# Short-sequence attention on one core: which queue issues the output stores, and when

## Chip, cores and metric

The kernel runs on one core of a Trainium2 chip. The metric is the device time of one execution in microseconds; the figure for a kernel is the median of several runs. A profile is of one single execution.

## What is computed

Batch 32, 12 heads, 128 positions, head size 64, all f32 in and out; 384 independent heads in all.

```
scale = 1.0 / np.sqrt(q.shape[-1])
scores = scale * np.matmul(q, k.transpose(0, 1, 3, 2))
attn = np.exp(scores - scores.max(-1, keepdims=True))
attn = attn / (attn.sum(-1, keepdims=True) + 1e-8)
return np.matmul(attn, v).astype(np.float32)
```

Three inputs of 12.58 MB each are read and one output of 12.58 MB is written.

## The kernel before

**Tiling.** The work is cut into 48 *units* of eight heads (NU, L32). Four units make a *super-unit* (supers, L35): 12 of them, numbered 0 to 11. For each super-unit there is one load of q, one of k and one of v, 1 MB of f32 each, turned into bf16 by the transfer (512 KB as written). q and k have four buffers each (NQ), v has two (NVB).

**A unit's way.** VectorE copies q or k into pairs of heads (pair_up, L248). TensorE transposes these (L174) and VectorE copies the transposes back (L257). TensorE puts v in order by matmuls with a selection matrix (order_v, "V", L188), and ScalarE copies that to SBUF (L234). TensorE makes the scores (L214), ScalarE the exponentials (L239), and TensorE multiplies by v, with a column of ones that gives the sums (L226). VectorE takes the reciprocal of the sums (L266) and multiplies (normalise, "N", L269), which leaves a unit's output in an o_sb tile of its own chunk; no o_sb tile is used twice.

**Order.** Each engine's instructions are laid down by hand in a list (program), and semaphores come from the dependencies. The steps in L409 to L434 run the units one behind the other in a software pipeline: step u has the V of unit u + 3, the scores of u + 1, the values of u and the N of u - 1.

**Loads.** All 36 loads are issued by GpSimd, in the order q, k, v of a super-unit (L436 to L446). Its queue is in order: an instruction that waits holds everything behind it. A q or k load waits until the buffer's last reader, four super-units ago, is done; a v load of super-unit x waits until V has read super-unit x - 2 (L387). Since the v load comes ahead of the next q and k in the queue, its wait paces all loads.

**Stores.** The 48 units' outputs are stored in 26 *chunks* (stores, L59): two chunks of one unit, 22 of two units, two of one unit. A chunk of two units is stored by two transfers (pieces, L351), so there are 48 store transfers of 256 KB each. The list own (L356) holds the chunks that GpSimd issues: before, those up to unit 33 (OWN = 34), 18 chunks and 34 transfers. The other eight chunks, 14 transfers, are issued by SyncE. A chunk of GpSimd's waits for the N of its last unit; one of SyncE's also waits for the N of unit 40 (HELD, L381). lane (L358) picks one of eight semaphores on which a chunk's transfers count their landing, four for each of the two issuers; SyncE waits for all eight at the end (L556).

**Where the stores stand in GpSimd's queue.** Behind each k load of super-unit x, chunks are added while the units stored so far, the next chunk's included, are at most MIXED * (x - 4) / 7 (L447, with MIXED = 24). So the first ones come with super-unit 5, and 24 units are stored ahead of the last v load. The rest of GpSimd's chunks follow behind the last load.

Of the kernel before, what the change touches and what calls it, by code (L numbers as in the profile page):

```python
# [10 lines left out]
def kernel(  # L11
# [23 lines left out]
    supers, u0 = [], 0  # L35
# [23 lines left out]
    stores = [1, 1] + [2] * ((NU - 4) // 2) + [1, 1]  # L59
# [26 lines left out]
    MIXED, OWN, HELD = 24, 34, NU - 8  # L86
# [267 lines left out]
        return 2 if 1 < stores[c] < supers[of_unit[first]][0] // 4 else 1  # L354

    own = [c for c in range(len(stores)) if sum(stores[:c + 1]) <= OWN]  # L356

    def lane(c):  # L358

        return c % 4 + (4 if c in own else 0)  # L360

    def store(c):
        name = "POOL" if c in own else "SP"
        e = ENGINE[name]
        n = stores[c]
        first = sum(stores[:c])
        R, f = supers[of_unit[first]]
        J = R // 4

        def emit():  # L370
            dst = o_rows[:, 2 * f:2 * f + 2 * J, :].rearrange("p (a w) e -> p a w e", a=2)[
                :, :, first - f:first - f + n, :]
            src = o_sb[c][:].rearrange("p (a w e) -> p a w e", a=2, w=n)
            if pieces(c) == 1:
                e.dma_start(out=dst, in_=src).then_inc(s_o[lane(c)], 16)  # L375
            else:
                for a in range(2):
                    e.dma_start(out=dst[:, a], in_=src[:, a]).then_inc(s_o[lane(c)], 16)  # L378

        last = first + n - 1  # L380
        op(name, ("store", c), emit, [("N", last if c in own else max(last, HELD))])  # L381

    def pool_load(kind, x):
        deps = []
        if kind == "v":
            if x >= NVB:
                deps = [("V", sum(vgroups[:x - NVB + 1]) - 1)]  # L387
            n, first = vgroups[x], sum(vgroups[:x])
            op("POOL", ("load", kind, x), lambda: nc.gpsimd.dma_start(  # L389
                out=v_b[x % NVB][:, :n, :], in_=v_rows[:, first:first + n, :],  # L390
            ).then_inc(s_v[x % NVB], 16), deps)
            return
        R, f = supers[x]
        j = "qk".index(kind)
        rows, bufs, sm = ((q_rows, q_b, s_q), (k_rows, k_b, s_k))[j]
        if x >= NQ:
            deps = [("P", t) for t in t_order if t[0] == x - NQ and t[1] == j]
        n = f * 8 // R

        def emit():  # L400
            nc.gpsimd.dma_start(  # L401
                out=bufs[x % NQ][:], in_=rows[R][:, n:n + 2, :]).then_inc(sm[x % NQ], 16)

        op("POOL", ("load", kind, x), emit, deps)
# [39 lines left out]
    todo = list(range(len(stores)))  # L444
    for _, kind, x in loads:
        pool_load(kind, x)  # L446
        while kind == "k" and sum(stores[:todo[0] + 1]) <= MIXED * (x - 4) / (len(supers) - 5):  # L447
            store(todo.pop(0))
    for c in todo:
        store(c)  # L450
# [138 lines left out]
```

The softmax here doesn't subtract the row's maximum and nothing guards it: scores larger than these inputs give would overflow.

## Time and profile before

| | us |
|---|---|
| median of 5 runs | 134.71 |
| the runs | 132.42, 132.71, 134.71, 135.47, 135.12 |
| the profiled execution | 135.38 |
| its span, first to last instruction | 133.6 |

| engine | busy us | share of the span |
|---|---|---|
| TensorE matmuls | 95.5 | 71% |
| VectorE | 89.6 | 67% |
| ScalarE | 73.7 | 55% |
| GpSimd | 51.1 | 38% |

The page cuts the span into 40 slices of 3.34 us and gives the busy share of each in tenths. A transfer's issue has a start on the issuing engine, and a landing, when its semaphore has its full count; between them lie the waiting in the queue and the transfer itself. The medians from issue to landing are 11.6 us for q, 13.4 for k, 10.5 for v, 12.8 for GpSimd's stores and 5.1 for SyncE's. GpSimd issues its 36 loads and 34 stores at 0.71 to 0.82 us each; SyncE issues its 14 stores from 114.3 us on. The share of the DMA engines in windows can be above 1, since packets overlap on an engine.

### The profile page before, as it was taken

To read this page: it belongs to the slowest core of one execution; us is meant where nothing else is said; L and a number is where in the kernel's file an instruction comes from. 1 tells how busy PE (TensorE), PEld (TensorE's weight loads), DVE (VectorE), ACT (ScalarE), POOL (GpSimd) and SP (SyncE) were. 2 spreads that over 40 slices of the span, in tenths; PEclk is the share of its full clock that TensorE was granted. 3 is DMA by queue.
4 is the path that set the end of the run, shared out by engine and by line. 5 is a ranking of instruction groups with operands and counts; after the bars stand their busy time and mean duration, and the time that the engine had idled before them with its cause. 6 is when DMAs were issued, how large, how long until landed. Compare 5 with 4: busy or idle time off the path is not lost. (4 is left out here: it accounts for less than half of the span.)

```text
span 133.6 us, 6988 instructions
## 1 busy us (share of the span) xinstructions
PE 95.5 (71%) x3072; PEld 67.7 (51%) x3072; DVE 89.6 (67%) x204; ACT 73.7 (55%) x97; POOL 51.1 (38%) x75
## 2 busy tenths in 40 slices
PE   0035889999899989888499589887688578577400
PEld 0034466776676666656366367555455456354200
DVE  1144535998989979599279489699198398475520
ACT  0001536868776785754655574971853754779400
POOL 5930004224073490953700941935904980000000
PEclk9999999999999999999869999999999999999955
DMA  1999999999999999999999999999999999999960
GB/s 12 165 198 207 211 204 214 162 192 202 205 211 181 196 267 229 208 347 227 211 343 230 211 284 213 243 326 207 240 328 216 239 327 317 405 383 342 329 210 10
DMA packets 19400, 31.56 MB, mean 236 GB/s; under 512 B 1344, under 2 KB 11072, under 8 KB 19392
## 3 DMA queue, kind: packets, MB, share of 16 engines
q0 software_dynamic: 15584, 27.79, 97.1%
q1 hardware_dynamic: 3808, 3.67, 8.0%
q8 instruction: 4, 0.07, 0.2%
q14 instruction: 4, 0.03, 0.1%
HBM read 37.75 MB, written 12.58 MB: 377 GB/s over the span
## 5 line engine op out<-in xcount | busy, mean ns | idle before, releaser
L239 ACT ACTIVATE attnT<-s_ps 128x1024 bf16<-128x1024 f32 x48 | 49.4, 1029 | 0.4 <-PE s_ps L214 0.2
L234 ACT CAST v_e<-v_ps 128x512 bf16<-128x512 f32 x48 | 28.3, 589 | 38.3 <-PE v_ps L188 19.7
L174 PE MATMUL qk_ps<-ident,pair 128*128 128x128 bf16 x384 | 32.3, 232 | 15.3 <-PEq L467 15.3
L188 PE MATMUL v_ps<-v_b,sel 128*32 128x256 bf16 x768 | 31.9, 289 | 11.4 <-PEq L467 11.3
L257 DVE COPY qkT<-qk_ps 128x1024 bf16<-128x1024 bf16 x48 | 32.8, 684 | 5.5 <-PE qk_ps L174 4.5
L269 DVE TENSOR_TENSOR o_sb<-o_ps,recip 128x512 f32<-128x512 f32 x48 | 33.2, 691 | 1.7
L174 PEld LDWEIGHTS qk_ps<-ident,pair 128*128 128x128 bf16 x384 | 24.0, 103 | 19.9 <-issue 18.5
L389 POOL DMA_DIRECT2D v_b<-in_v_dram x12 | 9.3, 774 | 57.3 <-PE v_ps L188 57.3
L188 PEld LDWEIGHTS v_ps<-v_b,sel 128*32 128x32 bf16 x768 | 16.9, 99 | 18.0 <-issue 14.0
L226 PE MATMUL o_ps<-v_e,attnT 128*32 128x65 bf16 x1536 | 21.0, 196 | 4.2 <-PEq L467 3.6
L248 DVE COPY pair<-q_b 128x1024 bf16<-128x1024 bf16 x24 | 10.9, 453 | 18.2 <-DMA q_b<-in_q_dram 18.1
L378 POOL DMA_DIRECT2D out_dram<-o_sb x32 | 23.0, 733 | 0.0
L226 PEld LDWEIGHTS o_ps<-v_e,attnT 128*32 128x32 bf16 x1536 | 15.5, 97 | 10.1 <-issue 6.5
L214 PE MATMUL s_ps<-qkT 64*128 64x128 bf16 x384 | 19.7, 224 | 0.7 <-PEq L467 0.5
L214 PEld LDWEIGHTS s_ps<-qkT 64*128 64x128 bf16 x384 | 11.2, 96 | 11.2 <-issue 11.2
L266 DVE RECIPROCAL recip<-o_ps 128x8 f32<-128x8 f32 x48 | 9.7, 202 | 8.7 <-PE o_ps L226 8.1
L248 DVE COPY pair<-k_b 128x1024 bf16<-128x1024 bf16 x24 | 10.3, 427 | 1.4 <-DMA k_b<-in_k_dram 1.4
L401 POOL DMA_DIRECT2D q_b<-in_q_dram x12 | 8.7, 727 | 1.0 <-SPq L94 1.0
L401 POOL DMA_DIRECT2D k_b<-in_k_dram x12 | 8.7, 727 | 0.0
L234 ACT ACT_TABLE_LOAD x1 | 1.3, 1283 | 13.0 <-DMA v_b<-in_v_dram 13.0
L546 DVE COPY sel<-ident 128x128 bf16<-128x128 bf16 x2 | 0.4, 223 | 1.8 <-POOL ident L521 1.8
L375 POOL DMA_DIRECT2D out_dram<-o_sb x2 | 1.4, 730 | 0.0
(8 smaller groups left out, 1.4 us busy)
## 6 DMA issues: line engine op xcount, KB each, us to landing
out_dram<-o_sb POOLq DMA_DIRECT2D x34, 256.0 KB, 12.8
q_b<-in_q_dram POOLq DMA_DIRECT2D x12, 512.0 KB, 11.6
k_b<-in_k_dram POOLq DMA_DIRECT2D x12, 512.0 KB, 13.4
v_b<-in_v_dram POOLq DMA_DIRECT2D x12, 512.0 KB, 10.5
out_dram<-o_sb SPq DMA_DIRECT2D x14, 256.0 KB, 5.1
```

Of the source, the lines that this page charges most:

```text
L174: i = nc.tensor.transpose(p[:, :, r4, jj, :], x[:, r].rearrange("p a d -> p (a d)"), ident[:])
L188: x = nc.tensor.matmul(t[r4 * 32:(r4 + 1) * 32, i, :, :], lhsT=pick[:, w * nh + i, jv, :], rhs=v_b[g % NVB][:, :n, (4 * jv + r4) * D:(4 * ...
L214: i = nc.tensor.matmul(t[:, a, h, :], lhsT=x[p, 1, 4 * w + h, :], rhs=x[p, 0, 4 * w + h, :], start=True, stop=True)
L226: y = nc.tensor.matmul(t[h * SO:(h + 1) * SO, a, r * (D + 1):(r + 1) * (D + 1)], lhsT=x[:, a, h, r * SO:(r + 1) * SO], rhs=v_e[m % NVE][:, ...
L234: return nc.scalar.copy(v_e[m % NVE][:, :, :D], v_ps[:].rearrange("p (n e) -> p n e", e=D))
L239: return nc.scalar.activation(out=attnT[u % NA][:].rearrange("p a h (r s j) -> p (a h r) s j", r=4, j=J), in_=s_ps[u % 2][:].rearrange("p ...
L248: return nc.vector.tensor_copy(pair[t_index[t] % NP][:], src[:, 8 * b:8 * b + 8])
L257: return nc.vector.tensor_copy(x.rearrange("p h (r j s) -> p (h r) j s", r=4, j=J)[:, :, 2 * b:2 * b + 2, :].rearrange("p x j s -> p x (j ...
L266: nc.vector.reciprocal(r[:], o4[:, :, :, D]).then_inc(s_r, 1)
L269: return nc.vector.tensor_mul(o[:, :, w, :].rearrange("p a (r d) -> p a r d", d=D), o4[:, :, :, :D], r[:].unsqueeze(3).to_broadcast([128, ...
L378: e.dma_start(out=dst[:, a], in_=src[:, a]).then_inc(s_o[lane(c)], 16)
L401: nc.gpsimd.dma_start(out=bufs[x % NQ][:], in_=rows[R][:, n:n + 2, :]).then_inc(sm[x % NQ], 16)
```

## The change

Two edits. In own, every second chunk behind the last that GpSimd already has is added, without the last two chunks: these are the chunks numbered 19, 21 and 23, with units 36-37, 40-41 and 44-45. They go from SyncE's queue to the end of GpSimd's, wait for their own units alone, and count on GpSimd's semaphores. In the loop that puts stores among the loads, the bound becomes MIXED * (x - 3) / 8.

```diff
     own = [c for c in range(len(stores)) if sum(stores[:c + 1]) <= OWN]
+    own += range(own[-1] + 2, len(stores) - 2, 2)
...
     for _, kind, x in loads:
         pool_load(kind, x)
-        while kind == "k" and sum(stores[:todo[0] + 1]) <= MIXED * (x - 4) / (len(supers) - 5):
+        while kind == "k" and sum(stores[:todo[0] + 1]) <= MIXED * (x - 3) / (len(supers) - 4):
             store(todo.pop(0))
```

The store transfers in GpSimd's queue behind the k load of each super-unit:

| k load of super-unit | 4 | 5 | 6 | 7 | 8 | 9 | 10 | 11 | behind the last load |
|---|---|---|---|---|---|---|---|---|---|
| before | 0 | 2 | 4 | 4 | 2 | 4 | 4 | 4 | 10 |
| after | 2 | 4 | 2 | 4 | 2 | 4 | 2 | 4 | 16 |

GpSimd then issues 40 store transfers and SyncE 8.

## The prediction

> **What bounds the kernel now.** I read the slices first, then the DMA queues, then the waits, then the tail in finer windows. From the page:
>
> ```profile
> PE   0035889999899989888499589887688578577400
> DVE  1144535998989979599279489699198398475520
> DMA  1999999999999999999999999999999999999960
> GB/s 12 165 198 207 211 204 214 162 192 202 205 211 181 196 267 229 208 347 227 211 343 230 211 284 213 243 326 207 240 328 216 239 327 317 405 383 342 329 210 10
> ...
> q0 software_dynamic: 15584, 27.79, 97.1%
> q1 hardware_dynamic: 3808, 3.67, 8.0%
> ...
> HBM read 37.75 MB, written 12.58 MB: 377 GB/s over the span
> ```
>
> No compute engine holds a 9 throughout; the DMA row does, from the second slice to the 38th. GB/s counts bytes as written, so a load that turns f32 into bf16 shows half of what it reads: about 205 in load stretches is 410 read. Two slices of the first fifteen stand lower, 162 and 181. The second holds the interval that matters. GpSimd issued the k load of super-unit 4 at 30.8 us, landing 11.3 later (42.1); the next load, v of super-unit 4, was issued at 37.5 and landed 7.9 later (45.4). Those lie 3.3 us apart, where the q and k behind them (38.3 + 9.7 and 39.0 + 11.4) land 2.4 apart. So about **0.8 us** of transfer time went unused near 44 us: the queue ran dry. Finer windows of 0.2 us show rates of 133 to 179 GB/s there. Behind 45 us every group of loads has stores queued with it and v landings take 9.1 to 12.7 us: never dry again. Waits from 45 to 114.5 us:
>
> ```profile
> POOL v_b L389 <- PE v_ps L188: 31.8, 7, 7.6
> ACT v_e L234 <- DMA v_b<-in_v_dram: 17.6, 8, 3.1
> DVE pair L248 <- DMA q_b<-in_q_dram: 12.5, 7, 2.7
> ```
>
> The compute engines wait for landings; GpSimd waits only for the v buffer, never for a store's data. The last v load (issued 102.0, landing 12.4 later) ends the loads at 114.4, and ScalarE had idled 2.75 us for it. The rest takes 13.6 us, to the last VectorE multiply, which ends at 128.04. SyncE issues the last store at 128.1, landing 3.8 later (131.9); the span ends 1.7 after that. The last 4 us, in windows of 0.1 us:
>
> ```profile
> DMA  9941111000699999972000000000000000000000
> GB/s 328 338 144 41 51 51 41 21 31 20 236 358 358 348 348 338 358 267 62 31 20 20 21 31 20 31 20 20 31 21 20 31 20 20 31 20 0 0 0 0
> ```
>
> After most of the last store has gone (129.8), a trickle of 20 to 31 GB/s runs to 131.6: about one sixteenth of the rate above it, so one DMA engine with a backlog of 1.8 us. It also trickled at 128.3 to 129.0 while the others had nothing. **Two ends lie close together**: the compute tail behind the last v, and that engine's queue, which sets the end.
>
> **What the Trainium skill says.** "DMA: Bandwidth & Descriptors", section "Issuing engines are not separate DMA queues": transfers from SyncE and GpSimd run on the same 16 engines, and a second issuer saves only issue time. The trace agrees: the DMA row is 9 with GpSimd alone and when SyncE joins at 114.3. Its section "Latency and other measured facts" says that engines 7 and 15 are usually slower, its cause a guess; the trace shows one late engine, not which. Its section "Queues, rings and completion order" says that an engine takes turns between queues packet by packet: hence a SyncE store overtakes GpSimd's queue, while GpSimd's own stay in order. The trace fits: SyncE's store issued at 124.8 landed in 2.7 us, GpSimd's of 109.1 in 13.9.
>
> **The change, part by part.**
>
> *Stores among the loads.* Removed: nothing. Moved: GpSimd's first 24 store transfers. Counted behind the k load of super-units 4 to 11 they were 0, 2, 4, 4, 2, 4, 4, 4 and become 2, 4, 2, 4, 2, 4, 2, 4: in total ahead of the last v load, 24 both times. Summed up, 2 more stand ahead behind the k of 4, 4 more behind that of 5, 2 more behind those of 6 to 9, none from 10 on. Each costs GpSimd 0.72 us; it has 3.3 to 7.6 us of wait per group, which hides it (without that cover, at most 4 x 0.72 = 2.9 us in a group). Their data is old enough: the first two need units 0 and 1, long finished at 31.6 us; the two issued behind super-unit 11 are counted against units up to 23, while PE is past the V of unit 35. No new wait.
>
> In the transfer queue a store takes 262 KB / 405 GB/s = 0.65 us (the rate at 114.5 to 117.4 us, GpSimd's stores alone). The two early ones, 1.3 us, come behind k of 4 and fill the 0.8 us gap. The v of 4 and the q and k of 5 then land 1.3 - 0.8 = 0.5 us later; the v of 5 and the q and k of 6, with 4 more ahead, 4 x 0.65 - 0.8 = 1.8 later; from the v of 6 to the k of 10, with 2 more ahead, 0.5 later. From the v of 10 on the same bytes are ahead, so these come **0.8 us earlier**, the last v too. The lateness costs compute waiting, nothing at the end, if the queue does not run dry and compute catches up: the 2.75 us of idling before the last v shrinks by at most 0.8 + 0.5, leaving 1.4. Worth: -0.8 us on the compute tail and on the late engine's queue. Bounds: 0 if the dry spell moves elsewhere, -1.3 if the two stores fill all of their length.
>
> *Stores in turns.* The chunks of units 36-37, 40-41 and 44-45, 6 transfers, go from SyncE to GpSimd. SyncE keeps 8. GpSimd gets a new wait for each; behind the one for unit 37 stand only the other two chunks, and nobody waits for those but the end. Unit 37's multiply ends at 108.0, GpSimd is busy with its ten stores to 109.8, so no wait: these go out at 109.8 to 111.2 instead of 116.0 and 117.2, behind the last v in its queue, which they don't delay. The next pair goes at 117.8 (unit 41) instead of 120.8, the last at 124.8 (unit 45), as now. Issue on GpSimd is 1.45 us a pair, hidden, since it has nothing else; the second of the last pair leaves at 125.5. If GpSimd's own delay to the first packet is as at the start (issued 1.5, first packets near 3.1), it moves by 127.2 to 128, within the backlog. SyncE's issues took up to 1.22 us each and its chunk of units 40-41 was late by 3.1 (117.7 to 120.8); that goes, but transfers were queued on the engines, so it gains nothing by itself.
>
> What it can gain is transfer efficiency: SyncE's stores move at 347 GB/s in 120 to 125 us, 0.755 us each, against 0.65. Six times the difference is 0.65 us. Part of that lower rate is lack of work, so bounds are 0 and -0.65; below nothing not excluded: the larger packets of GpSimd's queue beside SyncE's could cost +0.3. I take half, **-0.3**.
>
> *Sum.* -0.8 - 0.3 = -1.1 us. The late engine then ends at 131.6 - 1.1 = 130.5. The compute limit is 127.3 for the last issue plus the shortest landing seen, 2.7: 130.0, so the engine still decides, just. Span 133.6 - 1.1 = 132.5; the profiled execution, 135.38, becomes 134.3. The median of the five runs, 134.71, lies 0.7 below the profiled one; on it the change gives **133.6**.
>
> **Rivals.**
> 1. *Faster, the backlog dissolves.* If GpSimd's earlier store issues also take off the 1.8 us lag of the one engine, the end falls onto compute: 0.8 plus that lag, 2.6 us, and with the 0.65 in full up to 3.2: 131.5 to 132.1. For: the lag is visible, and SyncE was late with chunks. Against: work on an engine is conserved, and the shortest landing leaves only 1.9 us of room. The spread of the five runs, 132.42 to 135.47, is as large as this.
> 2. *Slower, the loop of loads runs dry.* A q load is issued when PE frees the v buffer and its landing feeds VectorE; later loads delay V, and that delays the next issue. If at each of the six v loads from 5 to 10 the queue is empty when v is issued, each costs a gap like the early ones (0.8 us): 6 x 0.8 = 4.8, less 1.1: +3.7, 138.4. It decides once a v landing falls below about 8 us, as the one with the gap (7.9). Against: landings are 9.1 to 12.7 now and the stores add to what is queued.
> 3. *No gain.* The dry spell reappears, or the end is fixed by the late engine in another way: 134.7. That the edit does nothing is excluded by the count of issues: 40 and 8 for 34 and 14.
>
> **How the numbers follow.** Forecast, 133.6, own range 132.8 to 134.4: 0.56. Rival 1, 131.8: 0.20; no gain, 134.7: 0.10; slower, 138.4: 0.14. The range leaves out most of the slower case and the edge of the faster: **131.3 to 135.5**. The bound of 2% (about what a measurement of this kernel can tell from no change) is 132.0 and 137.4. Faster: of rival 1 0.17, and 0.13 of the forecast's and no-gain's cases through the spread: 0.30. Slower: 0.13 of rival 2 and 0.01: 0.14. Within: 0.56.
>
> **What would show it.** Right: GpSimd issues stores from about 31.6 us; v of super-unit 4 lands near 45.9, without a dry stretch before it; the last v lands near 113.6; ScalarE's wait before it stays over 1 us; the last trickle ends near 130.5. Wrong: v landings of 8 us or less behind 45 us; a store on GpSimd that waits for VectorE ahead of a load; the last v at or behind 114.4; SyncE's last landing over 4 us after its issue.

## The result and the profile after

The changed kernel takes **134.15 us** in the median of 42 runs, the kernel before 133.79 in the median of 79. The ratio is **1.0036, 95% interval 1.0013 to 1.0059**: 0.13 to 0.59% slower, where 0.8% faster was forecast. The ratios, here and below, leave out the executions that lie more than 1.5% above their kernel's fastest, and the medians do not. The profile after is of an execution of 132.62 us (span 130.8), that of before of one of 135.38 us (133.6). Single runs of both kernels lie anywhere from 132 to 136 us, so the two spans must not be subtracted; what can be compared is where things lie inside each.

The page of the changed kernel, in the same slices as before:

```profile
PE   0034959899898788569988568788599988578510
DVE  1163357899989959717979829959748898764540
DMA  1999999999999999999999999999999999999872
GB/s 9 168 206 206 212 207 212 193 212 203 209 212 281 212 257 317 204 239 258 212 298 277 207 274 225 211 338 224 205 279 220 214 346 282 405 390 368 312 265 78
...
q0 software_dynamic: 16064, 29.36, 101.6%
q1 hardware_dynamic: 2176, 2.10, 4.7%
```

The slice at 40 us, 181 GB/s before, is now 281: stores are among the loads there. GpSimd's queue carries 29.36 MB instead of 27.79. The waits from 45 to 114.5 us are of the same kind and size as before:

```profile
POOL v_b L390 <- PE v_ps L188: 32.5, 6, 6.3
ACT v_e L234 <- DMA v_b<-in_v_dram: 16.9, 8, 3.7
DVE pair L248 <- DMA q_b<-in_q_dram: 11.9, 6, 3.2
```

GpSimd's issues at the end, from its timeline (start, time, what, and in brackets the wait ahead of it):

```profile
102.70 0.76 POOL L390 DMA_DIRECT2D v_b<-in_v_dram  x1 [5.35 <-PE v_ps L188]
103.44 8.51 POOL L379 DMA_DIRECT2D out_dram<-o_sb  x12
116.59 1.42 POOL L379 DMA_DIRECT2D out_dram<-o_sb  x2 [4.63 <-DVEq L479]
123.58 1.42 POOL L379 DMA_DIRECT2D out_dram<-o_sb  x2 [5.58 <-DVEq L479]
```

That is as the prediction had it: chunk 19 without a wait behind the ten, 21 and 23 behind their units. The last 4 us, from 127 us on, in windows of 0.1 us, have no trickle in this execution:

```profile
DMA  9997369999999200000000000000000000000000
GB/s 348 348 328 215 113 215 348 358 348 338 348 358 307 82 0 0 0 0 0 0 0 0 0 0 0 0 0 0 0 0 0 0 0 0 0 0 0 0 0 0
```

Transfers are over at 128.4, the last store (issued 126.6) lands 2.2 us later, at 128.8. Yet the span ends at 130.8, 2.0 behind that, where before it was 1.7. What lies there are the instructions with which each engine closes the block: a drain (DRAIN), the last of its own instructions, and then a semaphore (EVENT_SEMAPHORE) on which the engines wait for each other. Here are those of GpSimd and SyncE (count, least/median/greatest duration in ns, first to last start in us):

```profile
L516 POOLq DRAIN  x1: 5399/5399/5399, 124.0 to 124.0; - x1
L516 SPq DRAIN  x1: 7/7/7, 129.0 to 129.0; - x1
L516 SPq EVENT_SEMAPHORE  x1: 17/17/17, 129.6 to 129.6; - x1
```

SyncE is done at 129.0 and then waits 0.6 us for the others. GpSimd's closing drain ends at 124.0 + 5.4 = 129.4, behind the last landing. (Its record begins before GpSimd's last issue, at 124.3, so only its end is used here.) Before, it had ended at 106.4 + 18.4 = 124.8, 7 us ahead of SyncE's last landing:

```profile
L515 POOLq DRAIN  x1: 18351/18351/18351, 106.4 to 106.4; - x1
L515 SPq DRAIN  x1: 7/7/7, 132.2 to 132.2; - x1
L515 SPq EVENT_SEMAPHORE  x1: 17/17/17, 132.3 to 132.3; - x1
```

### The profile page after: what moved, and what is told of

It is laid out like the page before. It is cut to its first block, busy times and chain, and to the rows that moved or that the text cites. A ratio compares the mean times of both kernels' runs of the same rounds, so it can differ in the third digit from the quotient of the medians.

```text
span 130.8 us, 6988 instructions
## 1 busy us (share of the span) xinstructions
PE 94.7 (72%) x3072; PEld 67.4 (52%) x3072; DVE 90.1 (69%) x204; ACT 73.8 (56%) x97; POOL 55.3 (42%) x81
## 3 DMA queue, kind: packets, MB, share of 16 engines
q0 software_dynamic: 16064, 29.36, 101.6%
## 5 line engine op out<-in xcount | busy, mean ns | idle before, releaser
L234 ACT CAST v_e<-v_ps 128x512 bf16<-128x512 f32 x48 | 28.3, 589 | 36.3 <-PE v_ps L188 18.0
L379 POOL DMA_DIRECT2D out_dram<-o_sb x38 | 27.3, 734 | 10.2 <-DVEq L479 10.2
L248 DVE COPY pair<-k_b 128x1024 bf16<-128x1024 bf16 x24 | 10.5, 436 | 0.0
L376 POOL DMA_DIRECT2D out_dram<-o_sb x2 | 1.4, 730 | 0.0
```

Of the source, the lines that this page charges most:

```text
L234: return nc.scalar.copy(v_e[m % NVE][:, :, :D], v_ps[:].rearrange("p (n e) -> p n e", e=D))
L248: return nc.vector.tensor_copy(pair[t_index[t] % NP][:], src[:, 8 * b:8 * b + 8])
```

## The experiments

All ratios are to the kernel before, measured beside it on the same chip, with their 95% intervals. Each kernel had 22 runs, e2 had 12, m1 19, m2 6 and m3 14; w0 to w2 had one each.

**The edits one at a time, and the first one doubled.** e1 has the line in own alone; e2 the new bound alone; e3 this bound:

```diff
-        while kind == "k" and sum(stores[:todo[0] + 1]) <= MIXED * (x - 4) / (len(supers) - 5):
+        while kind == "k" and sum(stores[:todo[0] + 1]) <= MIXED * (x - 2) / (len(supers) - 3):
```

> Edit 'stores in turns' alone; the stores among the loads stand as before. Theory A (both edits gain, as predicted): ratio to before about 0.998. Theory B (turns cost what the early stores gain): about 1.008 to 1.010, with later landings of the last stores than before. Theory C (the early stores' gain doesn't exist, turns cost a little): about 1.003.

> Edit 'stores begin with super-unit 4' alone; the stores behind unit 34 stay with SyncE. Theory A and theory B: 0.994 (0.8 us off). Theory C: 1.000, within 0.003, with the dry stretch near 44 us filled and yet no earlier end. Theory D (early stores delay loads and that is not made good): 1.003 or more.

> The dose of the early stores doubled: they begin with super-unit 3, bound MIXED * (x - 2) / 9; no turns. If unused transfer time early is worth time at the end (A, B): 0.988 to 0.992. If not (C): 1.000. If early stores cost (D): 1.005 or more.

> The changed kernel again, on the chip and among the runs of the other three: 1.0036 as measured, and what its single edits must add up to. All theories: 1.001 to 1.006; its profile shows whether the early landings of the first profile after (last v at 112.9 us) come back or belong to that one execution.

| kernel | median us | ratio | interval |
|---|---|---|---|
| before | 133.82 | | |
| e1 turns only | 135.09 | 1.0016 | 0.9979 to 1.0054 |
| e2 early stores only | 133.56 | 0.9925 | 0.9883 to 0.9968 |
| e3 earlier still | 133.36 | 0.9997 | 0.9957 to 1.0037 |
| e4 the change | 134.27 | 1.0017 | 0.9981 to 1.0053 |

The two edits point in opposite directions in the medians, early stores down, turns up by 1.3 us; the ratio of e1 alone does not exclude 1. It does exclude the 1.008 of theory B. Theory D falls: early stores do not cost. For the early stores A and B foretell the same, and e2 and e3 disagree about it: e2 fits A and B, e3, with the doubled dose, fits C. The single edits do not add up either: multiplied, e1 and e2 give 0.994, and the change itself has 1.0017. In the profile of e4 the last v landed at 114.2 us, so the 112.9 of the first profile after belonged to that one execution.

The profile of e1 suggests why the early stores' gain is so unsteady. e1 issues the same things as before up to the last load, yet it has no dry stretch to fill. The DMA share and GB/s from 26 to 46 us, in windows of 0.5 us, first before, then e1:

```profile
DMA  9998999999999999999999999999999999999999
GB/s 164 199 207 117 193 205 201 221 213 201 201 217 223 164 201 205 186 207 203 215 209 203 225 201 221 205 201 225 180 160 172 184 186 178 205 170 199 211 199 209
```

```profile
DMA  9999999999999999999999999999999999999999
GB/s 203 217 217 207 213 209 217 209 201 221 205 182 190 199 207 213 205 223 215 201 217 201 233 205 205 209 197 209 205 205 209 209 211 227 201 217 201 217 217 201
```

Before dips to 117, 164 and 160; e1 never falls under 182. In e1 the k load of super-unit 4 (issued 30.2, landing 10.5 later) and the next v (36.3 and 6.9) land at 40.7 and 43.2, 2.5 us apart: back to back. The difference starts earlier, on TensorE. The matmuls of V between 18 and 19 us (count, busy us, mean ns), before and in e1:

```profile
L188 PE MATMUL v_ps<-v_b,sel 128*32 128x256 bf16 x16 | 1.0, 414 | 0.0
```

```profile
L188 PE MATMUL v_ps<-v_b,sel 128*32 128x256 bf16 x16 | 0.6, 275 | 0.0
```

In e1 they run at 275 ns from 15.2 us on, in the profile of before only from about 22 us. If V is late, so are the v buffer and the next v load (the third was issued at 21.9 us before, at 20.4 in e1), and the queue can run dry. The Trainium skill ("TensorE: Matmul & The Clock Gate", section "Part 1: The HAM clock gate (the "warmup" mystery)") has TensorE start at half clock, and the moment of release vary from run to run, since it hangs on a window that runs freely. The slow and the fast matmuls agree with the first. As to the second, the page gives half a microsecond either way for matmuls back to back; here the two moments lie over 6 us apart, in work with gaps, and what else moves them is not shown. At any rate the predicted gap is not there in every execution.

The other profiles point the same way. In six of the 17 kernels' profiles (without w0 to w2) V ran at some 275 ns for good before 20 us, and five of these executions took 132.1 to 133.0 us (after, e1, h1, k3, m3; h3 took 134.4). In the other eleven it did so only behind 20 us, and nine of these took 133.75 to 135.63 us (e3 took 133.0, h4 132.6). This goes across kernels and is an association, not a cause shown; but the two means lie 1.4 us apart, and the change itself is worth 0.5.

**An attempt to start TensorE's clock early.** To take this scatter out I put work on TensorE ahead of its loop: 64 transposes of the identity (w0), or 14 or 22 matmuls of 512 columns (w1, w2). Their results are never read.

```diff
+        nc.tensor.wait_ge(s_id, 1)
+        for _ in range(64):
+            nc.tensor.transpose(qk_ps[:, :128], ident[:], ident[:])
```

> The kernel before with 64 transposes of the identity put ahead of TensorE's loop (their result is never read), so that TensorE works from about 3.5 us on instead of from 7.8 us. In the profiles so far TensorE's matmuls of V take 421 ns up to a moment between 15.2 and 22 us and 273 ns behind it, and the executions in which that moment came late (21 to 22 us) are those that show dry stretches of the load queue near 27 and 44 us. Theory W (the late release of TensorE's clock makes the dry stretches): V at about 273 ns from its first at 13 us, the third v load issued at 20.5 us or earlier, landings of v at 28.3, 35.8, 43.3 us with no dry stretch, span 130 to 131.5. Rival: the clock falls back in the gaps before 20 us, or the dry stretches come all the same; then the warm start is no tool for separating the two edits.

> The kernel before with 14 matmuls of 512 columns ahead of TensorE's loop (identity by the selection matrix into v_ps, which the loop overwrites), some 28 instructions instead of 128, so that the loop's first instructions are not pushed into a later instruction fetch, which is what we take the first warm start's 10.7 us of TensorE idling (10.0 to 20.7 us, nothing awaited in the profile) for. They run from about 4 to 10 us. Theory W: the loop starts by 10.2 us, V takes 273 ns from 13 us on, third v load issued by 20.5 us, no dry stretch, span 130 to 131.5. Rival: the clock falls back before 16 us since TensorE is idle most of 10 to 13 us; then V takes 421 ns again at 13 to 16 us.

> The same with 22 such matmuls, to about 12 to 13 us, that is until k of the first super-unit has landed[...]. Theory W: V at 273 ns from its first, third v load by 20.5 us, no dry stretch, span 130 to 131.5. Rival: as for the one with 14, or the first transposes, 3 to 4 us late, cost what the clock brings.

All three failed as tools: 145.09 us for w0 beside 132.86 of the kernel before, 138.84 and 142.38 for w1 and w2 beside 135.25, each from one execution. TensorE's timeline in w0 and in w1:

```profile
3.51 6.51 PE L503 MATMUL qk_ps<-ident 128*128 128x128 bf16 x64 [3.51 <-POOL ident L524]
20.68 1.03 PE L174 MATMUL qk_ps<-ident,pair 128*128 128x128 bf16 x8 [10.67 <-PEq L467]
```

```profile
3.91 5.85 PE L504 MATMUL v_ps<-sel,ident 128*128 128x512 bf16 x14 [3.91 <-DVE sel L551]
10.71 0.61 PE L175 MATMUL qk_ps<-ident,pair 128*128 128x128 bf16 x8 [0.95 <-PEq L468]
12.20 0.61 PE L175 MATMUL qk_ps<-ident,pair 128*128 128x128 bf16 x8 [0.88 <-PEq L468]
16.29 1.01 PE L175 MATMUL qk_ps<-ident,pair 128*128 128x128 bf16 x8 [3.48 <-PEq L468]
```

The clock did rise (0.61 us for eight transposes at 10.7, where the cold ones take 1.01), and was down again at 16.3. Between, TensorE idled 10.67 us in w0 and 3.48 in w1, while the data of the next transposes were there from 8.0 us in w0 and from 13.9 in w1. What did come late were instructions. The trace has packets of 16 KB on a DMA queue of their own, "instruction", among the loads. One ended at 18.8 us in w0 and TensorE went on at 20.7; one ended at 14.6 in w1 and it went on at 16.3. All seven stretches of over 1.2 us that TensorE idles between the added work and 30 us in the three profiles end 1.7 to 1.9 us behind such a packet. No run isolates this, but it fits each time. So w0 to w2 changed more than the clock, and the link from clock to dry stretch is read from profiles and not shown by a controlled run.

**The turns on a base with early stores.** The base is e3's bound. h1 adds the turns (19, 21, 23), h3 all six chunks of units 34 to 45, h4 chunk 19 alone; h2 is the base.

```diff
+    own += range(own[-1] + 2, len(stores) - 2, 2)   # h1
+    own += range(own[-1] + 1, len(stores) - 2)      # h3
+    own += [own[-1] + 2]                            # h4
```

> Stores from super-unit 3 on (bound MIXED * (x - 2) / 9) plus the turns behind unit 34. This base has the narrowest spread of runs so far, so it shows a small effect of the turns best. To be compared with its control of the same call. Theory T (stores at the end cost more from GpSimd than from SyncE): 0.3 to 0.6% over the control. Theory U (the turns do nothing that can be measured): within 0.2% of the control. Theory V (as predicted, denser packets): 0.2% under it.

> Control: stores from super-unit 3 on, no turns; again the kernel of the doubled dose of early stores. All theories: median 133.3 us, ratio to before 0.995 to 1.000, few runs above 134.2.

> Doubled dose of the turns on the same base: all twelve transfers of units 34 to 45 go to GpSimd, SyncE keeps the last two. Theory T: 0.6 to 1.2% over the control. Theory U: within 0.2%. Theory V: 0.4% under it.

> Only the chunk of units 36 and 37 of the turns, on the same base: its two transfers go at about 110 us from GpSimd, queued right behind the others, instead of 115 to 117 from SyncE. If that early queueing is what costs (or helps), it has the whole effect of the turns; if the two chunks issued during the last units do, it equals the control within 0.2%.

| kernel | median us | ratio | interval |
|---|---|---|---|
| before | 134.01 | | |
| h1 base + turns | 133.72 | 0.9940 | 0.9896 to 0.9985 |
| h2 base | 132.66 | 0.9934 | 0.9900 to 0.9968 |
| h3 base + twelve transfers | 133.83 | 0.9984 | 0.9946 to 1.0023 |
| h4 base + chunk 19 | 132.60 | 0.9951 | 0.9914 to 0.9989 |

Chunk 19 changes nothing that can be told; theory V (denser packets gain) finds no support. h1 and h3 have medians some 1.1 us above the base, though h1's ratio is that of the base (one of h1's runs took 255.21 us, which neither figure feels). In the profiles, the time that SyncE waits at the block's end for the other engines was 0.2 us in h2 and h4, 0.5 in h1 and 0.3 in h3. This pointed to GpSimd's drain, though a wait of 0.1 us more, as in h3, is far from 1.1.

**Which chunk, and the drain by itself.** On the same base: chunks 19 and 21 (k1), 23 alone (k2), the base (k3), and the last two chunks, 24 and 25 (m1). On the change: without 23 (k4, again as m3), and the change itself beside it (m2).

```diff
+    own += [own[-1] + 2, own[-1] + 4]               # k1, k4, m3
+    own += [own[-1] + 6]                            # k2
+    own += [len(stores) - 2, len(stores) - 1]       # m1
```

> Super-unit 3 base with chunks 19 and 21 on GpSimd, 23 back on SyncE. Theory F (GpSimd's closing drain, which ends 2.0 to 2.4 us behind the last packet of GpSimd's own queue, and with chunk 23 ends 0.3 to 0.6 us behind the kernel's last landing): without chunk 23 the drain ends some us before the last landing; no cost, within 0.2% of the control or better. Theory T (every transfer moved to GpSimd near the end costs): 0.3% over the control.

> Super-unit 3 base with chunk 23 alone on GpSimd, two transfers. Theory F: the whole cost of the turns, 0.2 to 0.5% over the control, drain ending 0.3 to 0.6 us behind the last landing, though only a third of the transfers are moved. Theory T: a third of the cost, 0.1 to 0.15%.

> Control of this call: stores from super-unit 3 on, no turns. All theories: ratio to before 0.993 to 0.998, GpSimd's drain over 5 us ahead of the last landing.

> The changed kernel with chunk 23 given back to SyncE (stores from super-unit 4, chunks 19 and 21 on GpSimd). Theory F: it loses the changed kernel's cost and keeps the early stores' gain: ratio to before 0.994 to 0.998 against 1.002 to 1.004 of the changed kernel. Theory T: 1.000 to 1.002.

> Super-unit 3 base with only the last two chunks (units 46 and 47, one transfer each) on GpSimd: the strongest dose of the closing drain. Theory F: the span ends 3 us or more behind the last landing instead of 1.6 to 1.7, the drain ending about 1.8 us behind it; some 1.2% over the base, ratio to before 1.005 to 1.010. Theory T or an even cost per transfer: 0.1 to 0.2% over the base, ratio 0.994 to 1.000.

> The changed kernel beside the same without chunk 23, on one chip. All theories: ratio 1.001 to 1.005 to before.

> The changed kernel without chunk 23, second time. Theory F: 0.3 to 0.8% under the changed kernel of this call, ratio to before 0.994 to 0.999. If chunk 23 costs nothing (as in its single trial on the other base): equal to the changed kernel within 0.2%.

| kernel | median us (before) | ratio | interval | SyncE's wait at the end, us |
|---|---|---|---|---|
| k1 base + 19, 21 | 133.40 (134.14) | 0.9992 | 0.9958 to 1.0027 | 0.2 |
| k2 base + 23 | 133.19 (134.14) | 1.0022 | 0.9985 to 1.0059 | 0.3 |
| k3 base | 133.58 (134.14) | 1.0014 | 0.9972 to 1.0057 | 0.2 |
| k4 change without 23 | 133.22 (134.14) | 0.9980 | 0.9945 to 1.0016 | 0.2 |
| m1 base + 24, 25 | 134.53 (134.07) | 1.0070 | 1.0031 to 1.0110 | 1.5 |
| m2 change | 135.14 (134.07) | 1.0133 | 1.0056 to 1.0210 | 0.7 |
| m3 change without 23 | 133.74 (134.07) | 1.0015 | 0.9965 to 1.0066 | 0.2 |

m1 is the clear case. Two transfers moved, and the end of the profile reads:

```profile
L516 POOLq DRAIN  x1: 5135/5135/5135, 127.3 to 127.3; - x1
L516 SPq DRAIN  x1: 7/7/7, 131.1 to 131.1; - x1
L516 SPq EVENT_SEMAPHORE  x1: 17/17/17, 132.6 to 132.6; - x1
```

SyncE, which waits for every landing, is through at 131.1; GpSimd's drain ends at 132.4, and the block ends behind it. The ratio, 1.0070, compares with 0.9934 to 1.0014 of the base itself in the other comparisons (e3, h2, k3); the base was not measured beside m1. In m3, the change without chunk 23, the drain is over at 126.2 and SyncE waits for nothing:

```profile
L516 POOLq DRAIN  x1: 9957/9957/9957, 116.2 to 116.2; - x1
L516 SPq DRAIN  x1: 7/7/7, 129.8 to 129.8; - x1
L516 SPq EVENT_SEMAPHORE  x1: 17/17/17, 129.9 to 129.9; - x1
```

SyncE's wait is 0.2 us in the profiles of all nine kernels of this study's comparisons that keep chunks 23 to 25 on SyncE (before, e2, e3, h2, h4, k1, k3, k4, m3), and 0.3 to 0.7 in all seven with chunk 23 on GpSimd (after 0.6, e1 0.4, e4 0.3, h1 0.5, h3 0.3, k2 0.3, m2 0.7). That the drain ends the kernel in these is shown: from the last landing to the end of the span it is 1.65 us in each of the nine, 1.75 to 2.2 in the seven and 3.1 in m1. Its price in m1 came out as foretold in size.

For chunk 23 the price is small. k2 is within its error of k3, against the 0.2 to 0.5% that I expected. The change and its variant without chunk 23, side by side, are apart: 1.0133 (six runs) against 1.0015, intervals that overlap a little; 0.7 - 0.2 = 0.5 us of that difference of some 1.5 is the drain. In the three pairs that differ by all three chunks (e1 to before, e4 to e2, h1 to h2) the ratio rises by 0.0016, 0.0092 and 0.0006, which is 0.5 us on average with errors as large, and SyncE's wait by 0.2 us on average. **The rest is not explained.** Nor is it to be found at the end of the profiles. From the last multiply to the end of the span it takes 4.0 to 5.8 us in the seven with chunk 23 on GpSimd, mean 4.4, and 3.9 to 5.6 in the nine, mean 4.8. SyncE's last store landed sooner with chunk 23 gone from its queue, 2.1 to 2.7 us after its issue in six of the seven, against 2.1 to 3.8 in the nine, and that outweighs the drain. A cause that lies earlier was not looked for by any run, and the forecasts of the noise itself were off: h2 has 0.9934 against 0.995 to 1.000, k3 1.0014 against 0.993 to 0.998, m2 1.0133 against 1.001 to 1.005, m3 1.0015 against 0.994 to 0.999. The same base lay 0.8% apart from one comparison to the other.

## Why the prediction was wrong

- **Bound by transfers, little slack: right.** The DMA row is 9 nearly to the end in both, and 24 transfers ahead of the last v did not hurt: ScalarE waited 2.6 us for it after, 2.75 before, so compute had caught up.
- **The first step, -0.8 us for the dry stretch: the mechanism seen, the term mis-sized.** Filling the gap works in the profile after: the k of super-unit 4 lands at 30.3 + 11.0 = 41.3, two stores follow, and the v lands at 36.4 + 8.7 = 45.1, 3.8 later, which is two stores of 0.65 and a load of 2.5. But the 0.8 us was measured in one execution, and a long one. In e1's there was none. Single edits gave ratios from 0.9925 to 1.0014 in four trials (e2, e3, h2, k3), all four with a median below that of before, by 0.3 to 1.4 us. The mean of the four ratios, 0.9968, is 0.4 us, half of what I put down, and the four lie up to 0.9% apart.
- **The second step, "nobody waits for those but the end": the step that failed, as far as is known.** I priced GpSimd's late issues at nothing, "hidden, since it has nothing else", and followed the data to their landing. I left out that GpSimd must close too. Its drain ends 1.7 to 1.9 us behind the landing of its own last store, in before, after and m1, which no landing shows; with chunk 23 there, that is behind the kernel's last landing. In the three profiles of the changed kernel SyncE's wait for it was 0.6, 0.3 and 0.7 us, 0.33 more than the 0.2 of before. That is of the order of the 0.36% measured (0.5 us), but it does not settle it: the early stores' mean gain of 0.4 us would have covered it, and the last store landed sooner in most profiles. Why the change as a whole is slower stays open.
- **-0.3 us for denser packets: not seen.** Neither chunk 19 (h4) nor twelve transfers (h3) on the faster queue gained over h2. Chunks 19 and 21 (k1, 0.9992 beside 1.0014 of k3) leave room for a gain of that size, within the error. That larger packets beside SyncE's could cost up to 0.3 us, as the prediction allowed, was not tested by itself.
- **A wrong reading.** The store that was to show SyncE's overtaking GpSimd's queue, issued at 124.8 us, does not: GpSimd's queue had moved its last packet at 122.5. SyncE's first stores, issued from 114.3 on, moved nothing up to 117.4, while GpSimd's queue moved 1.18 MB from 114.5 on. From 117.5 to 122.5 both moved, SyncE's 1.45 MB and GpSimd's 0.35. The taking of turns from packet to packet, on which the prediction built, shows at best from there on.
- **Rivals.** The faster one (the trickle at the end dissolves) happened in the profile after, whose last store landed in 2.2 us instead of 3.8, and in e4, the same kernel, with 2.1; in m2, the same again, it took 3.5. It isn't dependable, and it did not make the kernel faster. The slower one, a queue that runs dry, did not happen: v landings stayed at 8.7 us and above from super-unit 4 on. The drain is a mechanism that I had not named among the rivals.
- **The signs, and luck.** All that was to show the prediction right was there in the profile after: stores from 31.0 us on, v of super-unit 4 at 45.1, the last v at 112.9, transfers over by 128.4. It was one execution, a short one, and the kernel was slower all the same. That the forecast time, 133.6, lies near the measured 134.15 is luck: it stood on a median of five runs, 134.71, which 79 runs put at 133.79.

The third rival, no gain, came nearest, though not for its reason. The start of the stores with super-unit 3 and no turns (e3, h2, k3) had a median below that of before in each of three comparisons, 133.36, 132.66 and 133.58 against 133.82, 134.01 and 134.14, and is the version I would keep; its ratio excludes 1 in one of the three, so that it beats the kernel before is likely and not settled.

## What to carry to other kernels

A transfer issued late in the program ends twice: when its data land, and when its issuer can close. Give the last transfers to the queue whose issuer closes soonest (here SyncE's), and read the closing drains in the profile before moving stores to an idle engine. A gap that is to be filled must be seen in more than one execution; where its origin is something that varies from run to run, a gain of its full size is not to be counted on.

## What the runs showed of the hardware that was not expected

- GpSimd's closing drain outlasts its own stores: its last one landed at 109.1 + 13.9 = 123.0 us before, at 124.3 + 3.2 = 127.5 after and at 127.3 + 3.4 = 130.7 in m1; the drain ended at 124.8, 129.4 and 132.4, that is 1.7 to 1.9 us later. Over all 17 kernels' profiles it is 1.6 to 2.1 us.
- TensorE's half clock comes back later, mostly for stretches of 3.4 us. In the 3.4 us ahead of three of them in e1 TensorE was busy for 1.3, 1.5 and 1.6 us. The third fell into the tail, at 114.2 to 117.6 us:

```profile
114.20:117.60 3.40, 3.40 (x96) 2.39 (x96) 1.59 (x3) 1.90 (x4) 1.42 (x2) 0.50 1.03 397
```

The columns are the stretch and its length, busy time of TensorE, weight loads, VectorE, ScalarE and GpSimd with counts, then granted clock (0.50), DMA share and GB/s. From the last v's landing at 112.3 to the last multiply it took 14.6 us there, against 13.6 in before. In four of the 17 profiles such a stretch fell just behind the last v (e1, h2, h3, k4), and the tail took 14.5 to 14.9 us; in the other thirteen it took 13.6 to 14.0.
- Code ahead of TensorE's loop delayed the loop far beyond its own time: 10.67 us of idling behind 6.51 us of transposes, ended 1.9 us behind a 16 KB packet of the instruction queue.
